# Retention's values and gates of three heads by a seven-product block scheme, the weight sums made by adding DMAs

## The chip, the cores and the metric

The kernel runs on one core of one Trainium2 chip. The metric is the device time of one execution in microseconds, as the median of several runs. A core has TensorE (PE in the profile), which multiplies; VectorE (DVE), ScalarE (ACT) and GpSimd (POOL), which work on tiles element by element; SyncE (SP), which here only issues DMAs; and 16 DMA engines that move data between HBM and on-chip memory. SBUF holds the tiles, PSUM the results of matmuls. Each engine works through its own instructions in program order and waits on semaphores for the others.

## What is computed

An encoder of four layers for one sequence of 512 tokens and a model width of 1024, float32. Layer i mixes tokens by latent attention (i = 0, 3), retention (1) or gated linear attention (2), and then runs a SwiGLU FFN; each sub-layer ends in a LayerNorm of alpha * x + y. The change touches retention alone, which occurs once, with 4 heads, query and key width 256, value and gate width 512:

```python
def retention_mixer(x, positions, w_in, decay_logit, gn_w, gn_b, w_o):
    proj = x @ w_in
    q = proj[..., : H * DK].reshape(B, S, H, DK)
    k = proj[..., H * DK: 2 * H * DK].reshape(B, S, H, DK)
    v = proj[..., 2 * H * DK: 2 * H * DK + H * DV].reshape(B, S, H, DV)
    g = proj[..., 2 * H * DK + H * DV:]
    q = apply_rotary(q, positions)
    k = apply_rotary(k, positions) * (DK ** -0.5)
    log_gamma = jax.nn.log_sigmoid(decay_logit)
    y = (retention_chunked(q, k, v, log_gamma[0], False)
         + flip_seq(retention_chunked(flip_seq(q), flip_seq(k), flip_seq(v), log_gamma[1], True)))
    y = (y - mean(y)) * lax.rsqrt(var(y) + LN_EPS)      # per token and head
    y = y.reshape(B, S, H * DV) * gn_w + gn_b
    return (jax.nn.silu(g) * y) @ w_o
```

The two chunked passes together weight the score of tokens n and m by a power of a decay, gamma^|n-m|, one gamma for each direction.

## The kernel before

**Precision.** Every large product is done in three matmuls. A float32 operand is kept as a pair: `hi`, its cast to the matmul's short float32 form, and `lo`, the rest. `split` (L100 to L102) makes a pair with two instructions, a cast on ACT (L101) and a subtraction on DVE that needs the cast (L102). `mm3` (L124 to L128) adds hi·hi (L126), hi·lo (L127) and lo·hi (L128) in one PSUM tile. A weight comes in pieces of 512 KB: `wload` issues the load into a `wraw` tile on SP's queue (L110; three such tiles) and `wsplit` splits it into `whi` and `wlo` (six tiles each). The layer's input is kept as the pair `xh`, `xl`. PSUM has six tiles for products (`ps`) and two for transposes (`tp`).

**Retention** runs head by head. Each head computes queries and keys (`queries_keys`, 96 matmuls of 128x512) and turns them by the rotary angles on DVE (`rope`, L787 to L789) with a split behind it; the values (`values`, 96 matmuls); the scores (`scores`, 24 matmuls in four tiles, m = 0 to 3, each evicted by one DVE instruction that multiplies by the decays, L863, and then split); the gate (`gate`, 96 matmuls, evicted by ACT with Silu, L876). `mix` multiplies scores and values (48 matmuls), normalizes each token on DVE and ACT, applies gn_w on DVE and gn_b and the gate on POOL (L902, L903). `turn` transposes the result (16 matmuls L910) and `out` multiplies it by the head's rows of w_o (96 matmuls), added to the running sum.

The heads overlap: head h's queries and keys come first, then `turn` of head h-1, values, scores, the decays of head h+1 (`decay`, L849 to L852), gate, mix and only then `out` of head h-1. Head 0 runs values, queries and keys, gate, scores, mix. Within this order a scheduler places each engine's instructions by priority, which is the order in which the code issues them, and by what is ready; `issue_after` holds a block of instructions behind a named one on the same engine. Tiles come from pools with a tag and a number of buffers; a new tile waits until an old one of the tag is read for the last time. The phase of a mixer (L1248) gives the number of buffers per tag; retention has the default, 47 tiles of tag `b` (128x512).

## Time and profile before

| | us |
|---|---|
| median of 3 runs | 2548.4 |
| lowest, highest | 2548.17, 2549.81 |
| the profiled execution's own time | 2547.14 |
| its span in the profile | 2545.4 |
| PE busy in the span | 2523.1 |
| DVE busy | 1771.1 |
| ACT busy | 975.5 |
| POOL busy | 200.9 |

The span is what the profile's records cover; the execution's own time is 1.7 us more. Mean granted clock of PE over the span: 0.998 of full speed. Busy times of different engines overlap. Retention with its output projection lies at about 588 to 1005 us.

### The profile page before, as it was taken

What the parts mean: (1) busy time and instruction counts of PE and PEld (TensorE: products, weight loads), DVE (VectorE), ACT (ScalarE), POOL (GpSimd) and SP (SyncE); (2) the same over time, 40 slices, a digit from 0 to 9 for tenths busy, and PEclk for the clock granted to TensorE, in tenths of its full rate; (3) what the DMA queues carried; (4) which work ended last, traced back from release to release, by engine and by line L of the source; (5) the groups of instructions that cost most, each with busy time, mean ns of one, the idle gap of its engine ahead of it and who ended that gap; (6) DMA issues with size and microseconds to landing.
All of it is one profiled execution on the core that took longest, in us unless ns stands there. A gap on an engine that the chain in (4) does not pass through costs nothing.

```text
span 2545.4 us, 32575 instructions
## 1 busy us (share of the span) xinstructions
PE 2523.1 (99%) x12804; PEld 2148.3 (84%) x12804; DVE 1771.1 (70%) x2988; ACT 975.5 (38%) x1405; POOL 200.9 (8%) x247
## 2 busy tenths in 40 slices
PE   8999999999999999999999999999999999999998
PEld 7888888888888888988888899988888888988887
DVE  6877666658755648666657878866657786666656
ACT  4752433323333332333333665233332564233331
POOL 2000111000100101111100000011100100011101
PEclk9999999999999999999999999999999999999999
DMA  4213333323222323333333222333332312333331
GB/s 153 71 42 104 100 100 99 100 83 108 75 83 76 99 83 100 104 95 100 108 100 88 90 69 75 113 100 99 100 92 76 96 57 64 102 100 99 100 91 58
DMA packets 294714, 232.35 MB, mean 91 GB/s; under 512 B 21121, under 2 KB 244481, under 8 KB 294561
## 3 DMA queue, kind: packets, MB, share of 16 engines
q1 hardware_dynamic: 294560, 230.28, 29.9%
q8 instruction: 100, 1.64, 0.3%
q14 instruction: 54, 0.43, 0.1%
HBM read 228.15 MB, written 2.10 MB: 90 GB/s over the span
## 4 chain that ended last, share of the span: by engine, by line
PE 94%; DVE 3%; ACT 1%; DMA 1%; issue 0%; POOL 0%; SPq 0%; DVEq 0%; ACTq 0%
PE ps L126 30%; PE ps L128 30%; PE ps L127 30%; PE tp L658 1%; PE tp L156 1%; DVE wlo L102 1%; PE ps L639 1%; PE ps L638 0%; ACT whi L101 0%; DMA wraw<-in_ret_w_in 0%; DMA wraw<-in_mla_w_down 0%; DMA wraw<-in_mla_w_uq 0%; ACT b L548 0%; DVE xt L203 0%; PE tp L910 0%
## 5 line engine op out<-in xcount | busy, mean ns | idle before, releaser
L101 ACT CAST whi<-wraw 128x1024 fp32r<-128x1024 f32 (+3 forms) x398 | 412.1, 1040 | 695.4 <-PE ps L127 231.8
L126 PE MATMUL ps<-xh,whi 128*128 128x512 f32 (+1 forms) x1792 | 657.2, 367 | 0.0
L127 PE MATMUL ps<-xl,whi 128*128 128x512 f32 (+1 forms) x1792 | 656.9, 367 | 0.1
L128 PE MATMUL ps<-xh,wlo 128*128 128x512 f32 (+1 forms) x1792 | 656.9, 367 | 0.0
L102 DVE TENSOR_TENSOR wlo<-wraw,whi 128x1024 fp32r<-128x1024 f32 (+3 forms) x398 | 488.6, 1237 | 212.3 <-ACT whi L101 204.3
L126 PEld LDWEIGHTS ps<-xh,whi 128*128 128x128 f32 x1792 | 337.8, 189 | 55.3 <-issue 0.4
L127 PEld LDWEIGHTS ps<-xl,whi 128*128 128x128 f32 x1792 | 338.1, 189 | 54.8 <-DVE lnx L139 0.3
L128 PEld LDWEIGHTS ps<-xh,wlo 128*128 128x128 f32 x1792 | 338.1, 189 | 54.6
L126 PE MATMUL ps<-whi,xh 128*128 128x512 f32 (+3 forms) x752 | 265.1, 353 | 0.7 <-ACT xh L101 0.7
L128 PE MATMUL ps<-whi,xl 128*128 128x512 f32 (+3 forms) x752 | 263.1, 350 | 1.4 <-DVE xl L102 1.4
L127 PE MATMUL ps<-wlo,xh 128*128 128x512 f32 (+3 forms) x752 | 262.8, 349 | 0.1
L180 DVE TENSOR_TENSOR xt<-ps,xt 128x512 f32<-128x512 f32 x288 | 187.4, 684 | 34.9 <-PE ps L128 34.9
L127 PE MATMUL ps<-wlo,fh 128*128 128x512 f32 x448 | 174.4, 389 | 0.0
L128 PE MATMUL ps<-whi,fl 128*128 128x512 f32 x448 | 174.4, 389 | 0.0
L126 PE MATMUL ps<-whi,fh 128*128 128x512 f32 x448 | 174.4, 389 | 0.0
L128 PEld LDWEIGHTS ps<-whi,xl 128*128 128x128 f32 x752 | 143.0, 190 | 19.4 <-DVE xl L102 2.4
L126 PEld LDWEIGHTS ps<-whi,xh 128*128 128x128 f32 x752 | 143.3, 191 | 18.4 <-ACT xh L101 1.1
L127 PEld LDWEIGHTS ps<-wlo,xh 128*128 128x128 f32 x752 | 143.3, 191 | 16.8 <-DVE wlo L102 0.4
L322 DVE TENSOR_TENSOR ft<-ps,b 128x512 f32<-128x512 f32 x64 | 44.2, 691 | 141.6 <-PE ps L128 78.0
L101 ACT CAST whi<-wt 128x1024 fp32r<-128x1024 f32 x64 | 67.5, 1054 | 191.0 <-PE ps L127 134.1
L325 POOL TENSOR_TENSOR ft<-ft 128x256 f32<-128x256 f32 x32 | 23.6, 737 | 1477.9 <-DVE ft L322 1477.9
L102 DVE TENSOR_TENSOR fl<-ft,fh 128x1792 fp32r<-128x1792 f32 x32 | 64.8, 2026 | 91.4 <-ACT fh L101 91.4
(257 smaller groups left out, 3985.5 us busy)
## 6 DMA issues: line engine op xcount, KB each, us to landing
wraw<-in_ffn_w_in SPq DMA_DIRECT2D x176, 512.0 KB, 3.9
wt<-in_ffn_w_out SPq DMA_DIRECT2D x48, 512.0 KB, 4.7
wraw<-in_ret_w_in SPq DMA_DIRECT2D x48, 512.0 KB, 4.0
wraw<-in_ffn_w_out SPq DMA_DIRECT2D x40, 512.0 KB, 3.3
wraw<-in_gla_w_in SPq DMA_DIRECT2D x22, 512.0 KB, 3.6
wraw<-in_mla_w_o SPq DMA_DIRECT2D x16, 512.0 KB, 3.8
wraw<-in_ret_w_o SPq DMA_DIRECT2D x16, 512.0 KB, 4.6
wraw<-in_mla_w_down SPq DMA_DIRECT2D x8, 512.0 KB, 4.3
```

The lines of the kernel that those rows point to most:

```text
L101: a = self.nc.scalar.copy(hi, src)
L102: b = self.nc.vector.tensor_tensor(lo, src, hi.bitcast(F32), op=ALU.subtract)
L126: mm(out, s[0], m[0], start=start, stop=False)
L127: mm(out, s[0], m[1], start=False, stop=False)
L128: mm(out, s[1], m[0], start=False, stop=stop)
L156: nc.tensor.transpose(ps[:, j, :], self.xt[t][:, (4 * g + j) * P : (4 * g + j + 1) * P], self.ident)
L180: nc.vector.tensor_tensor(x, ps, x, op=ALU.add)
L322: nc.vector.tensor_tensor(ft[:, 2:4, :] if f % 2 else ft[:, 1::-1, :], half(pu), half(s), op=ALU.mult)
L325: tt(ft[:, 4, :], ft[:, 0, :], ft[:, 3, :], op=ALU.add)
L639: nc.tensor.matmul(ps, qr[:, sl], krz[e], start=False, stop=True)
L658: nc.tensor.transpose(ps[:, kk, qq, :], pq[qq][:, k * P : (k + 1) * P], self.ident)
```

## The change

Values and gate of a head are one product of x (512 x 1024) with two column blocks of w_in (1024 x 512 each). The code after takes x as 2 x 2 blocks (tokens in halves a, the model width in halves c) and the weights as 2 x 2 blocks (values or gate, width half), and forms the result by the Winograd variant of Strassen's scheme: seven block products and a number of sums in place of eight products. Head 0 stays as it was.

- `factors` makes the sums of blocks of x once, during head 0, on DVE: ten additions or subtractions of 128x1024 in scratch tiles of the tag `t` (two buffers), and four splits into pairs of the tag `s`.
- `values_gate` makes seven `product`s. A product of a single weight block loads it as before into `wraw` tiles; one of a sum of blocks loads the first by SP into two `t` tiles and adds the others to them by DMAs from GpSimd. Its weight splits are held behind the eviction in `put_done`: that of score tile m = 2 for the first product, later that of the previous product's first half.
- Each product is 24 matmuls in two PSUM tiles, evicted by its `put` function: a copy on ACT, or additions on DVE, a split or Silu behind some.
- `out` of head h-1 becomes eight steps of 12 matmuls set between the products; in the last head four of them run behind `mix`, which is followed by the last head's own `out_last`.
- Scores now stand directly behind `turn`, without values between. `mix` works on pairs of token tiles with one `rsqrt_n` for two, and its two POOL operations are on DVE.
- Retention's phase has 30 tiles of tag `b`, 8 of `s`, 2 of `t`.

The core of the diff:

```diff
         def scores(h, q, k, gam):
...
+                if m == 2:
+                    self.put_done = i
...
         def mix(h, at, v, gs):
...
+            for t0 in (0, 2):
...
+                    nc.vector.tensor_tensor(y, y, gw, op=ALU.mult)
+                    nc.vector.tensor_tensor(y, y, gb, op=ALU.add)
+                    nc.vector.tensor_tensor(gs[t], gs[t], y, op=ALU.mult)
...
+        def factors():
...
+            def both(x, y):
+                d, e = scratch(), scratch()
+                tt(d, f32(x[0]), f32(y[0]), op=ALU.subtract)
+                tt(e, f32(x[1]), f32(y[1]), op=ALU.subtract)
+                tt(d, d, e, op=ALU.add)
+                return d
...
+            d = both(a21, a22)
+            s1 = keep(d)
+            for x in a11:
+                tt(d, d, f32(x), op=ALU.subtract)
+            s2 = keep(d)
+            for x in a12:
+                tt(d, d, f32(x), op=ALU.add)
+            s4 = keep(d)
+            return s1, s2, keep(both(a11, a21)), s4, a11, a12, a22
...
+            def product(blocks, s, put):
+                if len(blocks) == 1:
+                    ts = [self.wp.tile([P, 2, 512], F32, tag="wraw", name="wraw", bufs=self.nraw) for _ in range(2)]
+                else:
+                    ts = [self.b((P, 2, 512), name="wt", tag="t") for _ in range(2)]
+                for n, ac in enumerate(blocks):
+                    for c in range(2):
+                        if n:
+                            nc.gpsimd.dma_start(ts[c], block(ac, c), accum_op=ALU.add)
+                        else:
+                            nc.sync.dma_start(ts[c], block(ac, c))
+
+                with self.tc.issue_after(self.put_done.ins):
+                    ws = [self.wsplit(t, 2, 512) for t in ts]
+                for tt in range(2):
+                    ps = self.ps()
+                    for k in range(4):
+                        hi, lo = ws[k // 2]
+                        s2_ = tuple(x[:, k, tt * P : (tt + 1) * P] for x in s)
+                        self.mm3(ps, s2_, (hi[:, k % 2, :], lo[:, k % 2, :]), k == 0, k == 3)
+                    i = put(tt, ps)
+                    if tt == 0:
+                        self.put_done = i
...
+            steps = [
+                ([b21, b22, b12, b11], a22, keep("c21")),
+                ([b11], a11, keep("c11")),
+                ([b22, b12, b11], s2, put6),
+                ([b21], a12, put2),
+                ([b12, b11], s1, put5),
+                ([b22], s4, put3),
+                ([b12, b22], s3, put7),
+            ]
...
             else:
                 q, k = queries_keys(h)
                 yT = turn(gs)
-                v = values(h)
                 at = scores(h, q, k, gam)
                 gam = decay(h + 1) if h + 1 < RET_H else None
-                gs = gate(h)
...
+                v, gs, todo = values_gate(h, fac)
+                outs = out(h - 1, yT)
+                last = h == RET_H - 1
+                for step, n in zip(todo, (0, 0, 1, 1, 1, 1, 0) if last else (1, 2, 1, 1, 2, 1, 0)):
+                    step()
+                    for _ in range(n):
+                        outs.pop(0)()
             mix(h, at, v, gs)
...
-        with self.phase(**({}, {}, {"v": 8, "r": 4})[i % 3]):
+        with self.phase(**({}, {"s": 8, "t": 2, "b": 30}, {"v": 8, "r": 4})[i % 3]):
```

How the instructions stand on the engines is told below at three places; a row gives line, operation, output and inputs, and shape. Numbers behind names tell tiles of one name apart.

First, PE in head 1 behind k's projection. Before (`tp` are the transposes of head 0's result, `ps_6143` is the first tile of values):

```order
L910 MATMUL tp_6092<-ident_75,b_5684 128x128
L910 MATMUL tp_6092<-ident_75,b_5711 128x128
L126 MATMUL ps_6143<-whi_6121,xh_70 128x512
L127 MATMUL ps_6143<-wlo_6122,xh_70 128x512
L128 MATMUL ps_6143<-whi_6121,xl_71 128x512
L126 MATMUL ps_6143<-whi_6121,xh_70 128x512
```

After, the scores `ps_6123` and `ps_6136` stand there (`bh_5994`, `bl_5995` are the pair of q's first half, `bh_6074`, `bl_6075` that of k's, both from `rope`):

```order
L936 MATMUL tp_6096<-ident_75,b_5684 128x128
L936 MATMUL tp_6096<-ident_75,b_5711 128x128
L126 MATMUL ps_6123<-bh_5994,bh_6074 128x512
L127 MATMUL ps_6123<-bl_5995,bh_6074 128x512
L126 MATMUL ps_6136<-bh_5994,bh_6074 128x512
L127 MATMUL ps_6136<-bl_5995,bh_6074 128x512
L128 MATMUL ps_6123<-bh_5994,bl_6075 128x512
L128 MATMUL ps_6136<-bh_5994,bl_6075 128x512
L126 MATMUL ps_6149<-bh_5994,bh_6074 128x512
```

Values' matmuls, which needed only the layer's input and a weight, have gone from between the transposes and the scores.

Second, DVE at head 1's scores. Before (`b_6266` to `b_6305` are the four evictions, L863; `bl` behind each is its low part; `wlo` are weights for later products):

```order
L102 TENSOR_TENSOR bl_6256<-ps_6230,bh_6255 128x512
L863 SCALAR_TENSOR_TENSOR b_6266<-ps_6259,ret_g_5765 128x512
L102 TENSOR_TENSOR wlo_6610<-wraw_6607,whi_6609 128x1024
L102 TENSOR_TENSOR bl_6269<-b_6266,bh_6268 128x512
L863 SCALAR_TENSOR_TENSOR b_6279<-ps_6272,ret_g_5765 128x512
L102 TENSOR_TENSOR bl_6282<-b_6279,bh_6281 128x512
L863 SCALAR_TENSOR_TENSOR b_6292<-ps_6285,ret_g_5765 128x512
L102 TENSOR_TENSOR bl_6295<-b_6292,bh_6294 128x512
L863 SCALAR_TENSOR_TENSOR b_6305<-ps_6298,ret_g_5765 128x512
L849 TENSOR_SCALAR ret_g_6311<-ret_di_5202,rlg_5378 128x448 x2
```

After (the evictions are L880, `b_6130` to `b_6169`; `bl_6111` and `bl_6120` belong to the transposed result; `wlo_6196` and `wlo_6200` are the two halves of the first weight sum, from the `t` tiles `wt_6185` and `wt_6186`):

```order
L102 TENSOR_TENSOR bl_6111<-tp_6105,bh_6110 128x512
L102 TENSOR_TENSOR bl_6120<-tp_6114,bh_6119 128x512
L880 SCALAR_TENSOR_TENSOR b_6130<-ps_6123,ret_g_5765 128x512
L102 TENSOR_TENSOR bl_6133<-b_6130,bh_6132 128x512
L880 SCALAR_TENSOR_TENSOR b_6143<-ps_6136,ret_g_5765 128x512
L102 TENSOR_TENSOR bl_6146<-b_6143,bh_6145 128x512
L880 SCALAR_TENSOR_TENSOR b_6156<-ps_6149,ret_g_5765 128x512
L102 TENSOR_TENSOR wlo_6196<-wt_6185,whi_6195 128x1024
L102 TENSOR_TENSOR bl_6159<-b_6156,bh_6158 128x512
L880 SCALAR_TENSOR_TENSOR b_6169<-ps_6162,ret_g_5765 128x512
L102 TENSOR_TENSOR wlo_6200<-wt_6186,whi_6199 128x1024
L102 TENSOR_TENSOR bl_6172<-b_6169,bh_6171 128x512
```

The low part of the first weight sum now stands behind the third eviction. On PE, these rows are at the end of the scores (`ps_6162` is the fourth score tile, `ps_6245` one of `out`, `ps_6203` the first product):

```order
L126 MATMUL ps_6162<-bh_6003,bh_6083 128x512
L127 MATMUL ps_6162<-bl_6004,bh_6083 128x512
L128 MATMUL ps_6162<-bh_6003,bl_6084 128x512
L126 MATMUL ps_6245<-whi_6235,bh_6092 128x512
L127 MATMUL ps_6203<-wlo_6196,xh_70 128x512
L128 MATMUL ps_6203<-whi_6195,xl_71 128x512
L126 MATMUL ps_6203<-whi_6195,xh_70 128x512
L127 MATMUL ps_6203<-wlo_6196,xh_70 128x512
L128 MATMUL ps_6203<-whi_6195,xl_71 128x512
L126 MATMUL ps_6203<-whi_6199,xh_70 128x512
```

So the first product's second matmul, L127, needs `wlo_6196` from that place on DVE, and everything behind it on PE stands behind it.

Third, ACT at the end of head 0's gate. Before (`b_5711` is the gate's last Silu, `bh_5722` and `bh_5735` the first casts of head 0's scores):

```order
L101 CAST whi_6005<-wraw_6003 128x1024
L101 CAST whi_6036<-wraw_6034 128x1024
L101 CAST whi_6121<-wraw_6119 128x1024
L876 ACTIVATE b_5711<-ps_5686 128x512
L101 CAST whi_6127<-wraw_6125 128x1024
L101 CAST bh_5722<-b_5720 128x512
L101 CAST bh_5735<-b_5733 128x512
```

After:

```order
L101 CAST whi_6009<-wraw_6007 128x1024
L101 CAST whi_6040<-wraw_6038 128x1024
L101 CAST whi_6195<-wt_6185 128x1024
L895 ACTIVATE b_5711<-ps_5686 128x512
L101 CAST whi_6199<-wt_6186 128x1024
L101 CAST bh_5722<-b_5720 128x512
L101 CAST bh_5735<-b_5733 128x512
```

In place of weights that had come by plain loads, the casts of the two halves of head 1's first weight sum, `whi_6195` and `whi_6199`, stand around the last Silu and ahead of the score casts.

## Rows read from the trace of the kernel before

**Rows 1.** Page, parts 1 and 4: each engine's busy us, chain that ended last.

```profile
PE 2523.1 (99%) x12804; PEld 2148.3 (84%) x12804; DVE 1771.1 (70%) x2988; ACT 975.5 (38%) x1405; POOL 200.9 (8%) x247
...
PE 94%; DVE 3%; ACT 1%; DMA 1%; issue 0%; POOL 0%; SPq 0%; DVEq 0%; ACTq 0%
```

**Rows 2.** Windows, heads 1-3: us, PE, PEld, DVE, ACT, POOL, clock, DMA-share, GB/s.

```profile
674.00:779.00 105.00, 105.00 (x473) 87.06 (x472) 69.97 (x135) 37.46 (x47) 22.56 (x16) 1.00 0.21 66
779.00:884.00 105.00, 105.00 (x473) 87.05 (x472) 61.78 (x111) 34.71 (x44) 10.31 (x8) 1.00 0.30 90
884.00:990.00 106.00, 106.00 (x477) 87.93 (x476) 60.13 (x106) 32.18 (x41) 10.34 (x8) 1.00 0.29 90
```

**Rows 3.** Waits of PE, 640 to 1000 us, the largest: total, count, longest.

```profile
PE ps L126 <- ACT bh L101: 0.2, 1, 0.2
```

**Rows 4.** PE timeline, heads 0 and 1: start, us, engine, line, op, tiles.

```profile
663.87 0.50 PE L126 MATMUL ps<-bh 128*128 128x512 f32 x1
...
683.36 0.39 PE L126 MATMUL ps<-xh,whi 128*128 128x512 f32 x1
...
696.05 0.40 PE L128 MATMUL ps<-xh,wlo 128*128 128x512 f32 x1
696.29 1.04 PE L910 MATMUL tp<-ident,b 128*128 128x128 f32 x8
697.08 0.48 PE L126 MATMUL ps<-whi,xh 128*128 128x512 f32 x1
```

**Rows 5.** DVE timeline behind head 1's k; in brackets idle before, releaser.

```profile
696.49 0.69 DVE L788 TENSOR_TENSOR b<-ps,tab 128x512 f32<-128x512 f32 x1 [0.26 <-PE ps L128]
697.21 0.69 DVE L789 TENSOR_TENSOR b<-b 128x512 f32<-128x512 f32 x1
697.82 1.22 DVE L102 TENSOR_TENSOR wlo<-wraw,whi 128x1024 fp32r<-128x1024 f32 x1
699.56 0.69 DVE L787 TENSOR_TENSOR b<-ps,tab 128x512 f32<-128x512 f32 x1
700.16 0.68 DVE L788 TENSOR_TENSOR b<-ps,tab 128x512 f32<-128x512 f32 x1
```

**Rows 6.** Timeline of ACT, the same place.

```profile
697.94 0.62 ACT L101 CAST bh<-b 128x512 fp32r<-128x512 f32 x1 [0.59 <-DVE b L789]
```

**Rows 7.** Timeline of DVE at head 1's scores.

```profile
725.21 0.68 DVE L863 SCALAR_TENSOR_TENSOR b<-ps,ret_g 128x512 f32<-128x512 f32 x1
726.65 0.69 DVE L102 TENSOR_TENSOR bl<-b,bh 128x512 fp32r<-128x512 f32 x1 [0.76 <-ACT bh L101]
727.26 0.68 DVE L863 SCALAR_TENSOR_TENSOR b<-ps,ret_g 128x512 f32<-128x512 f32 x1
...
729.29 0.68 DVE L863 SCALAR_TENSOR_TENSOR b<-ps,ret_g 128x512 f32<-128x512 f32 x1
```

**Rows 8.** Timeline of PE early in layer 0, where it had stood still.

```profile
43.18 0.44 PE L531 MATMUL tp<-ident,b 128*128 128x128 f32 x2 [2.17 <-DVE b L525]
43.37 0.61 PE L127 MATMUL ps<-wlo,xh 128*128 128x512 f32 x1
...
46.77 0.49 PE L126 MATMUL ps<-whi,xh 128*128 128x512 f32 x1
```

**Rows 9.** Windows behind that gap and in head 0 (columns as in rows 2).

```profile
44.00:45.00 1.00, 1.00 (x3) 0.78 (x3) 0.94 (x2) 0.81 (x2) 0.03 (x1) 0.50 1.03 303
7.00:8.00 1.00, 0.93 (x2) 0.48 (x2) 1.00 (x2) 0.34 (x1) 0.00 (x0) 1.00 1.07 366
607.00:642.00 35.00, 35.00 (x156) 29.01 (x155) 28.04 (x63) 13.58 (x17) 0.00 (x0) 1.00 0.39 120
```

**Rows 10.** DMA view of the loads from ret_w_in, 512 KB each.

```profile
DMA to landing us min/median/max: 3.5/4.0/8.1
```

**Rows 11.** Timeline of SP's DMA queue, head 0: start, us, line, tiles, count.

```profile
632.62 29.74 SPq L110 DMA_DIRECT2D wraw<-in_ret_w_in  x6
```

**Rows 12.** Page, part 5: busy us, mean ns | idle before, releaser.

```profile
L101 ACT CAST whi<-wraw 128x1024 fp32r<-128x1024 f32 (+3 forms) x398 | 412.1, 1040 | 695.4 <-PE ps L127 231.8
```

More of the change, by code (lines that the diff above doesn't have):

```diff
@@ L862, in scores @@
                 a = self.b()
-                nc.vector.scalar_tensor_tensor(
+                i = nc.vector.scalar_tensor_tensor(
                     a, ps, RET_DK**-0.5, gam[:, 384 - m * P : 896 - m * P], op0=ALU.mult, op1=ALU.mult
@@ L916, in out, with step @@
         def out(h, yT):
-            last = h == RET_H - 1
-            if last:
-                self.ln_begin(l, 0)
-            st = lambda f, t: (yT[f][0][:, t * P : (t + 1) * P], yT[f][1][:, t * P : (t + 1) * P])
-            self.out_proj(st, wo[h * 512 : (h + 1) * 512], 4, ALPHA if h == 0 else None, last)
+            ch = {}
+            def step(t, hf):
+                if t == 0:
+                    rows = wo[h * 512 : (h + 1) * 512]
+                    ch[hf] = [self.wcols(rows, c * 256, 2, hf * 512, 512) for c in range(2)]
+                ps = self.ps()
+                for f in range(4):
+                    w2 = ch[hf][f // 2]
+                    sl = slice(t * P, (t + 1) * P)
+                    self.mm3(
+                        ps, (yT[f][0][:, sl], yT[f][1][:, sl]), (w2[0][:, f % 2, :], w2[1][:, f % 2, :]), f == 0, f == 3
+                    )
+                self.acc(t, hf, ps, ALPHA if h == 0 else None, False)
@@ new lines, in values_gate, with block, keep, put @@
+        def values_gate(h, fac):
+            rows = w.rearrange("(g a p) c -> g p a c", g=4, p=P)
+            s1, s2, s3, s4, a11, a12, a22 = fac
+            v, gs = [None] * NT, [None] * NT
+            tmp = {}
+            def block(ac, c):
+                c0 = 2048 + ac % 2 * 2048 + h * 512
+                return rows[2 * (ac // 2) + c, :, :, c0 : c0 + 512]
+            def product(blocks, s, put):
[7 more added lines that the diff above has]
+                            nc.gpsimd.dma_start(ts[c], block(ac, c), accum_op=ALU.add)
+                        else:
+                            nc.sync.dma_start(ts[c], block(ac, c))
+                with self.tc.issue_after(self.put_done.ins):
+                    ws = [self.wsplit(t, 2, 512) for t in ts]
+                for tt in range(2):
+                    ps = self.ps()
+                    for k in range(4):
[5 more added lines that the diff above has]
+                        self.put_done = i
+            tt_ = nc.vector.tensor_tensor
+            def keep(name):
+                def put(tt, ps):
+                    tmp[name, tt] = self.b()
+                    return nc.scalar.copy(tmp[name, tt], ps)
+                return put
+            def put_v(t, x):
+                v[t] = self.bpair()
+                self.split(*v[t], x)
+            def put6(tt, ps):
+                u = tmp["u", tt] = self.b()
+                tt_(u, ps, tmp["c11", tt], op=ALU.add)
+                x = tmp["c21", tt]
+                return tt_(x, x, u, op=ALU.add)
+            def put2(tt, ps):
+                x = tmp["c11", tt]
+                i = tt_(x, ps, x, op=ALU.add)
+                put_v(tt, x)
+                return i
+            def put5(tt, ps):
+                u = tmp["u", tt]
+                return tt_(u, ps, u, op=ALU.subtract)
+            def put3(tt, ps):
+                g = gs[tt] = self.b()
+                i = tt_(g, ps, tmp["u", tt], op=ALU.add)
+                nc.scalar.activation(g, g, AF.Silu)
+                return i
+            def put7(tt, ps):
+                x = tmp["c21", tt]
+                tt_(x, ps, x, op=ALU.add)
+                put_v(2 + tt, x)
+                g = gs[2 + tt] = tmp["u", tt]
+                i = tt_(g, g, ps, op=ALU.subtract)
+                nc.scalar.activation(g, g, AF.Silu)
+                return i
+            b11, b12, b21, b22 = range(4)
+            steps = [
[7 more added lines that the diff above has]
+            ]
+            return v, gs, [lambda a=a: product(*a) for a in steps]
@@ L931, in retention @@
                 at = scores(h, q, k, gam)
+                gam = decay(1)
+                fac = factors()
             else:
@@ L934, in retention @@
                 yT = turn(gs)
-                v = values(h)
                 at = scores(h, q, k, gam)
                 gam = decay(h + 1) if h + 1 < RET_H else None
-                gs = gate(h)
-            if h == 0:
-                gam = decay(1)
+                v, gs, todo = values_gate(h, fac)
[5 more added lines that the diff above has]
+                        outs.pop(0)()
             mix(h, at, v, gs)
-            if h:
-                out(h - 1, yT)
-        out(RET_H - 1, turn(gs))
+            if h == RET_H - 1:
+                for step in outs:
+                    step()
+        out_last(RET_H - 1, turn(gs))
     def gla(self, l, j):
```

67 lines of the change are left out of this document (48 added, 19 removed).

## The prediction

> **What bounds the kernel now.** I read the busy table and the chain of work first. TensorE (PE) is busy for 99% of the span, and the chain that ended last runs 94% over it [rows 1]; the reader should see that nothing else bounds the kernel on average. The change lies in retention's heads 1 to 3, so I then read those stretches: in 105 and 106 us PE is busy for 105.00 and 106.00, at full clock, with DVE at 60 to 70 and the DMA engines at a fifth to a third [rows 2]. In that stage PE's waits hold lines no larger than 0.2 us [rows 3]. Heads 1 to 3 are thus saturated on PE: fewer matmuls are worth their full price there, and so is any new wait. The price of one is a spacing, since matmuls overlap: from the start at 683.36 to that at 696.05 there are 56 intervals, (696.05 - 683.36) / 56 = 0.2267 us [rows 4].
>
> **Part 1, matmuls removed.** Values and gate of a head are 2 x 96 matmuls of 128x512. Seven products of 24 make 168, so 24 go per head and 72 in all. 72 x 0.2267 = 16.3 us, all on the path: **-16.3**.
>
> **Part 2, the scores lose their cover.** Before, PE had values' 96 matmuls (21.8 us) between the transposes of `turn` and the scores, and the gate's 96 behind them. Now the scores follow the transposes at once (first order rows of the change), and the first product needs `wlo` of a weight sum that DVE computes only behind the eviction of score tile m=2 (second order rows). I follow DVE from PE's last k matmul, taken as t=0 (696.28 in the trace). There DVE starts the k rope's second multiplication at +0.21 and the sum at +0.93; ACT casts from +1.66 to +2.28 [rows 5, 6]. PE has two groups of transposes meanwhile, 0.8 us (eight start at 696.29, the next matmul at 697.08 [rows 4]), then nothing: the first scores wait 1.4 to 1.5 us for the cast, taken as 1.4. From there DVE takes a 128x512 pass every 0.60 us [rows 5]: low part of k's first half until 2.9, three rope passes to 4.7, the cast to 5.6, its low part and two of the turned tiles' at 5.6 to 7.4, the other two turned tiles at 8.4 and 9.0 behind PE's remaining transposes. So score eviction m=0 starts at 9.6. One score tile costs DVE 2.04 us, because eviction, ACT's cast and the low part follow each other [rows 7]: m=1 at 11.65, m=2 at 13.7, then the weight's low part (1.22 [rows 5]) from 14.3 to 15.5. PE has in that time 16 transposes, 24 score matmuls (5.4 us) and two or three others for which its operands are there; it is through with them at about 9.2, but for one at 10.3. Idle: 15.5 - 9.2 - 0.2 = about 6.1 us, where before there was none.
>
> Then the clock. Behind a gap of 2.17 us early in the trace [rows 8] PE's granted clock is 0.50 (1.2 instead of 2.4 GHz) [rows 9], and the eight matmuls from 43.37 to 46.77 take (46.77 - 43.37) / 8 = 0.425 each, so 8 x (0.425 - 0.227) = 1.6 us more [rows 8]. I charge 1.6 to each long gap. DVE's weight split for `out`, behind the decay's passes, adds 0.3; with the first wait of 1.4: 6.1 + 1.4 + 1.6 + 0.3 = 9.4 per head, **+28.2** for three. Bounds: with the first wait covered and the tiles 0.5 us closer (two spacings, 1.1), 6.9 per head, 21; with one tile more in line before the split (2.04), 11.4 per head, 34.
>
> **Part 3, sums by the loads.** A sum of n blocks is one plain load and n-1 adding DMAs from GpSimd, on two `t` tiles at once. The trace shows no adding DMA. Let A be the time of one adding step of such a pair. Nearest rows: a plain 512 KB load lands in 4.0 us at the median and 8.1 at the longest [rows 10]. An adding DMA has twice the bytes to fetch; 512 KB at the highest throughput seen, 366 GB/s [rows 9], is 1.43 us, so 4.0 + 1.4 = 5.4 and I take A = 5.5, nearer to the median than to the longest since the engines are idle for two thirds here [rows 2]; the range uses A = 4.0 to 8.1. That an adding DMA is below a plain one I exclude: it does the load and more.
>
> The Trainium skill ("DMA: Bandwidth & Descriptors", Anatomy of one DMA — SWDGE (gpsimd) path) gives about 2 us plus the bytes at 436 GB/s; with the bytes doubled that would be an estimated 4.4 us, and the sum below would come to about +18 rather than +26. No run here shows a load from GpSimd.
>
> Where A matters:
> - Head 0 to head 1. The factors of x (ten sums, four splits: 14 DVE passes of 128x1024, 17 us at 1.22 [rows 5]) go to a stretch in which DVE is busy for 28.04 of 35 us [rows 9]; their scratch tiles are the `t` tiles, so these come free at about 637 and 642. The second tile's load is queued on SP behind a weight load (the third of six between 632.6 and 662.4, about 644 [rows 11]); it lands at 648.5. Three adding steps: 665 at A = 5.5. ACT's casts of both sums stand ahead of head 0's score casts (third order rows), so the mix, which began at 663.87 [rows 4], waits for 648.5 + 3A + 1.04 (cast of a weight [rows 12]) + 0.62 (score cast [rows 6]): 667.5, so +3.7, with the clock **+5.3**. At A = 4.0: 662.2, nothing. At 8.1: +10.6 + 1.6.
> - The three-block sum of product 3. Its tiles come free when product 1's split is done; in head 3, where `out` puts no steps there, only 47 matmuls (10.7 us) lie between. Load 4.0, 2A, split 2.2, against 10.7 plus the 0.6 of a pass: a wait of about 2A - 5.1. A = 5.5: 5.9 + 1.6 = **+7.5**. A = 4.0: 2.9 + 1.6. A = 8.1: 11.1 + 1.6. In heads 1 and 2 three `out` steps more (36 matmuls, 8.2 us) lie between: 2A - 12.6 at the most, nothing at 5.5, 3.6 each at 8.1.
> - Product 1 of heads 2 and 3 has some 21 us (72 matmuls, 16.3, and the mix's statistics) for a load and three steps before ACT's casts hold up the mix: 3(A - 5.7), nothing at 5.5, 7.2 each at 8.1.
>
> The Trainium skill (the same page, Issuing engines are not separate DMA queues) says that the transfers of all issuing engines share the same DMA engines, so by it two sums under way and the loads beside them would lengthen each other, toward rival R2. The trace has a DMA share of 0.2 to 0.3 there [rows 2], which leaves room.
>
> **Part 4, the rest.** The mix in pairs moves two passes from GpSimd to DVE (8 x 0.6 = 4.8 us a head; PE is then busy with 12 to 48 matmuls of `out` or the next q, which hide it; uncovered only before the last `turn`, where both tiles' passes stand in line: 1 us, taken with 0 to 2, v's split behind weight splits in it): **+1**. Plain loads stay 512 KB each.
>
> **Sum** at A = 5.5: 28.2 + 5.3 + 7.5 + 1 - 16.3 = +25.7. The profiled execution took 2547.14, the median of the runs is 2548.4, 1.3 above it; 2547.1 + 25.7 = 2572.8 in a profiled run, **2574** as a median.
>
> **Rivals.**
> - *R1, the chain of scores costs less and the change is not slower.* If PE's new idle time stays under 16.3 us in all, that is under 5.4 per head with nothing lost to sums, the matmuls decide. That takes DVE's line before the split to be some 4 us shorter than I have it (the rope's first passes done before k's last matmul, the tiles 0.5 us closer, the clock not falling), and A near 4. For it: DVE is idle for a third of these stretches [rows 2], so it may come to the line with less in hand than I assume. Against: each of the line's links hangs on the one ahead, and the order puts nothing else on PE. With 3 to 5 us per head it is 9 to 15 - 16.3 + 0 to 5 for sums: 2541 to 2552, about 2545.
> - *R2, adding DMAs as slow as the longest load.* A = 8.1: 28.2 + (10.6 + 11.1 + 7.2 + 14.4 + 1.6 x 6 = 52.9) + 1 - 16.3 = +66, **2614**. It decides from A = 5.7, where product 1's chain starts to hold up the mix. For: two at once, beside SP's loads. Against: the share of 0.3.
> - *R3, they cost what a load costs.* A = 4.0: 28.2 + 0 + 4.5 + 1 - 16.3 = +17.4, **2566**.
> - That the matmuls don't go away is no rival: the order lists 72 fewer.
>
> **How the numbers follow.** Within 0.2%, 5.1 us, counts as the same: 2543.3 to 2553.5. Forecast with A from 4.7 to 6 (2568 to 2590): 0.37. R3, with the score chain at its lower bound (2554 to 2568): 0.25. R2 (2590 to 2620): 0.18. R1: 0.20, of which 0.11 is faster and 0.09 the same. So faster 0.11, same 0.09, slower 0.80. For 8 in 10 I leave out R1's faster half and some of the rest (0.15 of it) and the top of R2 (0.05): 2551 to 2608.
>
> **What the profile after would show.** Right: matmuls fewer by 72; in heads 1 to 3 a gap of about 6 us on PE released by DVE's `wlo` from a `wt` tile, with a granted clock of 0.50 behind it; the same matmul spacing elsewhere. GpSimd's adding loads landing 5 to 6 us after the one before; ACT waiting on DMA with `whi` from `wt` at the end of head 0; a gap before product 3 in head 3. Wrong: gaps of under 3 us before product 1 (then Part 2 fails and R1 holds); landings at 4 or 8 (R3, R2); a gap that I have not named, such as evictions of products on DVE behind splits.

## The result, and the profile after

| | before | after |
|---|---|---|
| median, us | 2548.3 (4 runs) | 2705.14 (4 runs) |
| lowest, highest | 2548.17, 2549.81 | 2701.97, 2706.92 |
| span in the profile | 2545.4 | 2700.0 |
| mean granted clock of PE | 0.998 | 0.972 |

The changed kernel is slower by 157 us: a ratio of 1.0613, 95% interval 1.0594 to 1.0631. The prediction was slower, at 2574 in a range of 2551 to 2608; the time lies 97 us above the range. The sign was right and the size was not.

The page after, parts 1, 3, 4 and 6 (to be read against rows 1; `q0` is GpSimd's DMA queue with its packets, MB and share, and the last line gives the adding DMAs, KB each and median us from issue to landing):

```profile
PE 2553.7 (95%) x12732; PEld 2158.1 (80%) x12732; DVE 1826.3 (68%) x3038; ACT 997.3 (37%) x1437; POOL 209.2 (8%) x257
...
q0 software_dynamic: 11424, 22.02, 5.2%
...
PE 82%; DVE 6%; issue 5%; DMA 4%; ACT 3%; POOL 1%; SPq 0%; DVEq 0%; ACTq 0%; POOLq 0%
...
wt<-in_ret_w_in POOLq DMA_DIRECT2D x42, 512.0 KB, 6.2
```

PE has 72 instructions fewer, as the prediction's first step says, and yet 30.6 us more busy time: at the old speed it would have been 16.3 us less, so the matmuls took 46.9 us longer. Most of that is the clock. From 588 to 1180 us the mean granted clock is 0.88; by the trace's record of the clock, PE was busy there for 78.4 us at 0.50, the lower of its two levels, where before it was so for none. Half of it, 39 us, is the price; the other 8 us are not placed.

```profile
588.00:1180.00 592.00, 469.17 (x1952) 373.86 (x1951) 343.50 (x607) 170.19 (x219) 53.88 (x44) 0.88 0.50 122
```

The chain's share on PE fell from 94% to 82%, and DMA, ACT and "issue" came in. The waits of PE and of ACT in retention (588 to 1180 us), largest first, with total, count and longest, where before PE's line was 0.2 us [rows 3]:

```profile
PE ps L126 <- ACT bh L101: 49.2, 9, 24.7
PE ps L126 <- ACT whi L101: 31.7, 9, 11.6
PE ps L127 <- DVE wlo L102: 20.8, 10, 6.1
PE ps L126 <- ACT b L926: 15.5, 2, 8.4
```

```profile
ACT whi L101 <- DMA wt<-in_ret_w_in: 172.6, 21, 20.9
```

The line of ACT is the one to see: ACT stood 172.6 us before casts of weight sums whose DMA had not landed, and the casts of scores, values and mix stand behind them on ACT. That is why the longest wait in PE's largest line, 24.7 us, names `bh`, a score's cast, although no score was late by itself.

I added up all of PE's gaps of 0.3 us and more from 588 to 1180 us: 122.3 us. By what ended them, and where: the end of head 0, 25.0; ahead of products in heads 1 to 3, for a weight or its sum, 37.1; the scores, with the hold behind them, 31.3; the mix's evictions (L926), 15.5; the casts of values at the start of a mix, 12.0; the rest 1.4. With the 46.9 us of longer matmuls that is 169.2. The span grew by 154.6, and 16.3 of matmuls were saved, 170.9 together, so 1.7 us are not placed. The largest gap of each kind, and the clock behind one of them (columns as in rows 2):

```profile
688.34 0.79 PE L126 MATMUL ps<-bh 128*128 128x512 f32 x1 [24.67 <-ACT bh L101]
...
738.83 0.80 PE L127 MATMUL ps<-wlo,xh 128*128 128x512 f32 x1 [4.52 <-DVE wlo L102]
...
1005.85 0.80 PE L126 MATMUL ps<-xh,whi 128*128 128x512 f32 x1 [8.44 <-ACT b L926]
...
1066.23 1.22 PE L126 MATMUL ps<-whi,bh 128*128 128x512 f32 x2 [11.61 <-ACT whi L101]
```

```profile
739.00:740.00 1.00, 1.00 (x3) 0.81 (x4) 1.00 (x3) 0.00 (x0) 0.00 (x0) 0.50 0.13 18
```

And the cause, on GpSimd. Its timeline at the end of head 0 and later in head 1's mix; each row is the issue of one adding DMA of 512 KB:

```profile
661.49 1.21 POOL L1019 DMA_DIRECT2D wt<-in_ret_w_in  x1 [5.17 <-PE ps L128]
667.85 1.22 POOL L1019 DMA_DIRECT2D wt<-in_ret_w_in  x1 [5.15 <-issue]
674.14 1.20 POOL L1019 DMA_DIRECT2D wt<-in_ret_w_in  x1 [5.08 <-issue]
680.59 1.21 POOL L1019 DMA_DIRECT2D wt<-in_ret_w_in  x1 [5.25 <-DMA wt<-in_ret_w_in]
...
819.68 1.22 POOL L1019 DMA_DIRECT2D wt<-in_ret_w_in  x1 [7.54 <-issue]
825.99 1.21 POOL L1019 DMA_DIRECT2D wt<-in_ret_w_in  x1 [5.09 <-issue]
832.56 1.22 POOL L1019 DMA_DIRECT2D wt<-in_ret_w_in  x1 [5.35 <-issue]
```

They start 6.3 to 6.6 us apart, and the page gives 6.2 us from issue to landing: one starts when the one ahead is through. Of the 42, none starts before the one ahead has landed, and 30 start 0.25 to 0.45 us behind that landing. At 825.99 that isn't a wait of the program. This DMA adds to the first tile, whose last DMA was issued at 810.92 and landed at 819.36, and the one at 819.68, which landed at 825.68, is for the other tile; the idle time is put down to "issue". So two tiles were "under way" in the code, and one after the other on the chip. The DMA engines were not full in that time (DMA share 0.64, the last figure but one):

```profile
826.00:850.00 24.00, 19.96 (x83) 16.02 (x82) 4.07 (x16) 1.05 (x1) 4.87 (x4) 0.93 0.64 114
```

A step of a pair took 2 x 6.35 = 12.7 us, where the prediction took 5.5 and at most 8.1.

### The profile page after: what moved, and what is told of

It reads as the page before. It is cut to its first block, busy times and chain, and to the rows that moved or that the text cites. A ratio compares the mean times of both kernels' runs of the same rounds, so it can differ in the third digit from the quotient of the medians.

```text
span 2700.0 us, 32591 instructions
## 1 busy us (share of the span) xinstructions
PE 2553.7 (95%) x12732; PEld 2158.1 (80%) x12732; DVE 1826.3 (68%) x3038; ACT 997.3 (37%) x1437; POOL 209.2 (8%) x257
## 3 DMA queue, kind: packets, MB, share of 16 engines
q0 software_dynamic: 11424, 22.02, 5.2%
## 4 chain that ended last, share of the span: by engine, by line
PE 82%; DVE 6%; issue 5%; DMA 4%; ACT 3%; POOL 1%; SPq 0%; DVEq 0%; ACTq 0%; POOLq 0%
PE ps L126 26%; PE ps L127 26%; PE ps L128 26%; DMA wt<-in_ret_w_in 2%; DVE wlo L102 1%; PE tp L675 1%; DMA wraw<-in_ret_w_in 1%; ACT whi L101 1%; POOL wt L1019 1%; PE tp L173 1%; ACT bh L101 1%; DVE bl L102 1%; DMA wraw<-in_mla_w_down 0%; PE ps L656 0%; PE ps L655 0%
## 5 line engine op out<-in xcount | busy, mean ns | idle before, releaser
L126 PE MATMUL ps<-xh,whi 128*128 128x512 f32 (+1 forms) x1792 | 659.0, 368 | 15.5 <-ACT b L926 15.5
L127 PE MATMUL ps<-xl,whi 128*128 128x512 f32 (+1 forms) x1792 | 658.4, 368 | 0.1
L126 PEld LDWEIGHTS ps<-xh,whi 128*128 128x128 f32 x1792 | 338.6, 189 | 72.2 <-ACT b L926 16.3
L127 PEld LDWEIGHTS ps<-xl,whi 128*128 128x128 f32 x1792 | 339.1, 189 | 55.1 <-DVE lnx L139 0.3
L127 PE MATMUL ps<-wlo,xh 128*128 128x512 f32 (+3 forms) x632 | 220.2, 348 | 15.5 <-DVE wlo L102 15.4
L126 PE MATMUL ps<-whi,xh 128*128 128x512 f32 (+3 forms) x632 | 220.4, 351 | 7.7 <-ACT whi L101 7.0
L101 ACT CAST whi<-wt 128x1024 fp32r<-128x1024 f32 x88 | 92.6, 1052 | 363.6 <-DMA wt<-in_ret_w_in 172.6
L128 PE MATMUL ps<-whi,xl 128*128 128x512 f32 (+3 forms) x632 | 219.2, 347 | 2.3 <-DVE xl L102 2.3
L126 PE MATMUL ps<-whi,bh 128*128 128x512 f32 (+1 forms) x416 | 161.1, 388 | 27.7 <-ACT whi L101 24.7
L126 PE MATMUL ps<-bh 128*128 128x256 f32 (+1 forms) x376 | 129.6, 351 | 50.4 <-ACT bh L101 50.0
L127 PE MATMUL ps<-wlo,fh 128*128 128x512 f32 x448 | 174.3, 389 | 0.0
L102 DVE TENSOR_TENSOR wlo<-wt,whi 128x1024 fp32r<-128x1024 f32 x88 | 114.2, 1298 | 85.1 <-ACT whi L101 84.1
L127 PE MATMUL ps<-wlo,bh 128*128 128x512 f32 (+1 forms) x416 | 160.6, 386 | 5.4 <-DVE wlo L102 5.4
L128 PE MATMUL ps<-whi,bl 128*128 128x512 f32 (+1 forms) x416 | 158.7, 383 | 0.0
L127 PEld LDWEIGHTS ps<-wlo,xh 128*128 128x128 f32 x632 | 122.9, 194 | 30.2 <-DVE wlo L102 17.6
```

What stands on the lines that cost most here:

```text
L101: a = self.nc.scalar.copy(hi, src)
L102: b = self.nc.vector.tensor_tensor(lo, src, hi.bitcast(F32), op=ALU.subtract)
L126: mm(out, s[0], m[0], start=start, stop=False)
L127: mm(out, s[0], m[1], start=False, stop=False)
L128: mm(out, s[1], m[0], start=False, stop=stop)
```

## The experiments

"Measured" is one run, with the kernel before at 2547.5 to 2548.9 beside it, unless an interval is given. e1, e3 and e4 leave the additions out, e2 half of each sum; the others leave nothing out.

**What is slow about the sums: e1 to e4.** e1, plain loads in place of adding ones:

```diff
-                            nc.gpsimd.dma_start(ts[c], block(ac, c), accum_op=ALU.add)
+                            nc.gpsimd.dma_start(ts[c], block(ac, c))
```

> The same DMAs from GpSimd with the same waits, but as plain loads: the later blocks overwrite the first instead of being added to it, so the weight sums are left out of the computation. Theory A (one DMA from GpSimd holds GpSimd for its whole 6.3 us, whatever it does with the data, so the two tiles of a pair follow each other): starts of successive DMAs stay 6.2 to 6.5 us apart where the tiles are free, time within 10 us of 2705. Theory B (the adding makes them long and keeps them apart): spacing falls below 4 us and the time by 80 us or more, toward 2600.

Measured 2607.26. GpSimd's timeline:

```profile
651.10 1.47 POOL L1019 DMA_DIRECT2D wt<-in_ret_w_in  x2 [5.93 <-DMA wt<-in_ret_w_in]
...
797.62 0.73 POOL L1019 DMA_DIRECT2D wt<-in_ret_w_in  x1 [3.48 <-DMA wt<-in_ret_w_in]
798.90 0.72 POOL L1019 DMA_DIRECT2D wt<-in_ret_w_in  x1 [0.55 <-DMA wt<-in_ret_w_in]
```

Two loads are handed on in 1.47 us, back to back, with the same waits; theory A is out and B holds, though the time fell less far for it than with the sums away (e3): 37 us of waiting stay. Plain loads in place of adding ones save 2705 - 2607 = 98 us. One more thing changes with the adding: the same 22.02 MB go in 6048 packets here, against 11424 above. Per DMA that is 128 packets of 4 KB where an adding DMA has 256 of 2 KB, with 16 of 4 bytes beside them in either. So e1 alone does not tell the adding from the number of packets.

```profile
q0 software_dynamic: 6048, 22.02, 2.6%
```

What is left of the gaps on GpSimd is waiting for the DMA ahead on the same tile, as the program asks for.

e2, adding DMAs of half the size, the other half of each sum left out:

```diff
+                            nc.gpsimd.dma_start(ts[c][:, :1], block(ac, c)[:, :1], accum_op=ALU.add)
```

> Each adding DMA moves one of its two rows of 512 columns per partition, 256 KB instead of 512 KB; the other half of each sum is left out. Theory A1 (the time of a GpSimd DMA goes with the number of its pieces): spacing about 3.2 to 3.6 us, landing likewise; by the prediction's sum with a step of 2 x 3.4 = 6.8 us instead of 12.7 the time is about 2600. Theory A2 (most of the 6.3 us is a fixed cost of each DMA): spacing 5 us or more and a time above 2670.

Measured 2610.17, as A1 said, though not for its reason: the spacing isn't half, it is gone.

```profile
652.68 1.75 POOL L1019 DMA_DIRECT2D wt<-in_ret_w_in  x2 [6.45 <-DMA wt<-in_ret_w_in]
...
797.54 0.89 POOL L1019 DMA_DIRECT2D wt<-in_ret_w_in  x1 [3.34 <-DMA wt<-in_ret_w_in]
798.80 0.87 POOL L1019 DMA_DIRECT2D wt<-in_ret_w_in  x1 [0.38 <-DMA wt<-in_ret_w_in]
```

Two adding DMAs of 256 KB go out in 0.87 us each, as e1's loads do in 0.73, and what they wait for is the DMA ahead on the same tile. Landing takes 5.9 us at the median. These are adding DMAs of 128 packets, two at once at the most, and GpSimd does not hold them: it is not the adding by itself.

e3 leaves the additions out altogether, so each sum is its first block alone:

```diff
-                for n, ac in enumerate(blocks):
+                for n, ac in enumerate(blocks[:1]):
```

> The adding DMAs are left out, each sum is its first block alone. All other instructions stay. Theory A (the sums cost all that went past the forecast, the scores cost what Part 2 says): idle of PE at the scores of heads 1 to 3 about 7.5 us each, time 2547 + 28 + 1 - 16 = 2560. Rival C (the mix in pairs, evictions on DVE and held splits cost much by themselves): 2590 or more. Rival D (the scores' waits come from the sums too): 2540 to 2550.

Measured 2570.68. PE's gaps at head 1's scores:

```profile
698.15 0.50 PE L126 MATMUL ps<-bh 128*128 128x512 f32 x1 [1.29 <-ACT bh L101]
706.46 0.47 PE L126 MATMUL ps<-whi,bh 128*128 128x512 f32 x1 [1.10 <-DVE b L880]
711.46 0.79 PE L127 MATMUL ps<-wlo,xh 128*128 128x512 f32 x1 [4.53 <-DVE wlo L102]
```

6.9 us, and 6.9 and 7.4 in heads 2 and 3, where the prediction has 1.4 + 6.1. Theory A's 2560 is 11 us short, so it was right on these gaps and not on what lies around them: 6.1 us of smaller gaps (the mix's start, a late weight) and more half clock.

e4 is e3 with the first product's weight splits free of the hold:

```diff
+                if blocks == [b21, b22, b12, b11]:
+                    ws = [self.wsplit(t, 2, 512) for t in ts]
+                else:
+                    with self.tc.issue_after(self.put_done.ins):
+                        ws = [self.wsplit(t, 2, 512) for t in ts]
```

> As e3_nosum, and the first product's weight splits are no longer held behind the third score eviction. Part 2 of the prediction: the hold is the cause of the wait before the first product, so that wait goes, what is left of the scores' idle time is 1 to 2 us per head, and the time falls by 12 to 20 us against e3_nosum, to 2540 to 2548. Rival: the chain of score evictions is late anyway and the next product waits instead; then it falls by less than 5 us.

Measured 2559.02, 11.7 us below e3, just under what was expected of the hold. (The 2540 to 2548 in the expectation was reckoned from 2560 for e3, before e3 had run.) The gap of 4.5 us before the first product is gone in all three heads. A new one of 1.9, 1.9 and 4.6 us stands before the second product, whose split is held behind the first one's eviction:

```profile
715.70 0.85 PE L126 MATMUL ps<-whi,xh 128*128 128x512 f32 x2 [1.90 <-ACT whi L101]
```

**Other ways to make the sums: e5, e6, e12, e15.** e5 splits each adding DMA into two of 256 KB, nothing left out:

```diff
+                            for b in range(2):
+                                nc.gpsimd.dma_start(ts[c][:, b : b + 1], block(ac, c)[:, b : b + 1], accum_op=ALU.add)
```

> Each adding DMA of 512 KB is replaced by two of 256 KB on the two halves of the same data; nothing is left out. Theory P (an adding DMA of 512 KB alone is so long in pieces that GpSimd can't hand on the next until it is nearly through; one of 256 KB is handed on in 0.9 us, as e2_half showed): starts 0.9 to 1.5 us apart, a step of a pair 6 to 8 us, time 2605 to 2640. Theory Q (what holds GpSimd is the sum of pieces under way, so four of 256 KB are held up as two of 512 KB): the step stays near 12 us and the time above 2680.

Measured 2655.57, between the two theories. e2's 0.87 us hold only as long as few are under way; here four may be, and they don't:

```profile
810.57 0.89 POOL L1020 DMA_DIRECT2D wt<-in_ret_w_in  x1 [1.18 <-issue]
812.73 0.87 POOL L1020 DMA_DIRECT2D wt<-in_ret_w_in  x1 [1.27 <-issue]
815.67 0.86 POOL L1020 DMA_DIRECT2D wt<-in_ret_w_in  x1 [2.06 <-issue]
817.71 0.86 POOL L1020 DMA_DIRECT2D wt<-in_ret_w_in  x1 [1.18 <-issue]
```

Starts are 2.0 to 2.9 us apart, again by "issue". Counted over all 84 DMAs, from issue to landing, never more than three are under way: a fourth starts some 0.3 us behind a landing. So something under way is limited, not the single DMA. e12 cuts them once more, into four of 128 KB with rows of half the length:

```diff
+                                for d in range(2):
+                                    sl = slice(256 * d, 256 * d + 256)
+                                    nc.gpsimd.dma_start(ts[c][:, b, sl], block(ac, c)[:, b, sl], accum_op=ALU.add)
```

> As e5_halves with four adding DMAs of 128 KB in place of two of 256 KB, each of as many rows as before but of half the length. If the time of an adding DMA goes with its bytes: about 1 us each, time within 15 us of e5_halves' 2656. If it goes with its number of rows: about 2 us each as in e5, a step of a pair 16 us, time above 2705.

Measured 2699.91, 44 us above e5 and not within 15, and not above 2705 either: neither expectation came out whole. Starts are 1.3 us apart at the median, which looks like a limit by bytes. The count of DMAs under way says otherwise:

```profile
674.10 0.86 POOL L1022 DMA_DIRECT2D wt<-in_ret_w_in  x1 [0.29 <-issue]
675.28 0.89 POOL L1022 DMA_DIRECT2D wt<-in_ret_w_in  x1 [0.32 <-issue]
...
791.65 2.65 POOL L1022 DMA_DIRECT2D wt<-in_ret_w_in  x3 [5.46 <-DMA wt<-in_ret_w_in]
795.03 0.86 POOL L1022 DMA_DIRECT2D wt<-in_ret_w_in  x1 [0.72 <-issue]
```

From 791.65 three go out before any has landed, and the fourth, at 795.03, starts 0.31 us behind the first one's landing at 794.72. Over all 168 DMAs there are again never more than three under way, although each has half the bytes of e5's; 142 start with two others still under way. What the two runs share is the number of packets of a DMA, 144:

```profile
q0 software_dynamic: 12096, 22.03, 5.0%
q0 software_dynamic: 24192, 22.03, 5.6%
```

The first line is e5's, for 84 DMAs, the second e12's, for 168. So three DMAs of 144 packets may be under way (432), while a fourth (576) waits, and so does a second one of the changed kernel's 272 packets (544). Bytes don't order the runs: 768 KB are under way in e5, and in e12 512 KB are too many. Starts are closer in e12 because a DMA lands sooner, 4.2 us at the median against 6.6. In time this gains little: head 2's first sum takes 40.2 us from its first issue to its last landing in the changed kernel, 28.7 in e5 and 37.9 in e12, the order of the three times.

e15 is the changed kernel with four `t` tiles:

```diff
-        with self.phase(**({}, {"s": 8, "t": 2, "b": 30}, {"v": 8, "r": 4})[i % 3]):
+        with self.phase(**({}, {"s": 8, "t": 4, "b": 26}, {"v": 8, "r": 4})[i % 3]):
```

> The changed kernel with four t tiles instead of two, four tiles of tag b fewer, nothing else. If the cost of the sums is latency (GpSimd can't begin a sum until the one ahead has been split; its 14 DMAs x 6.35 us = 89 us per head would fit into a head), the waits for products 3, 5 and 7 go and only head 0's and the scores' stay: 2600 to 2650. If GpSimd's rate is the limit, above 2680.

Measured 2639.91, 65 us better and inside the first range. ACT's wait for sums falls from 172.6 to 44.4 us and the products' waits nearly go; what stays is the scores with their hold, head 0's end (10.8 us), and now 16.9 and 15.5 us at the mix of heads 1 and 2, where the casts of the next head's first sum stand ahead on ACT:

```profile
ACT whi L101 <- DMA wt<-in_ret_w_in: 44.4, 6, 10.7
```

```profile
815.24 0.80 PE L126 MATMUL ps<-bh 128*128 128x512 f32 x1 [16.89 <-ACT bh L101]
```

So 65 us of the loss came from sums that couldn't begin until two tiles were free, behind the split of the sum ahead or, at head 0, behind the scratch sums of `factors`; the length of each DMA is the same (e15's starts are 6.2 to 6.6 us apart too). What stays is the length of a sum and the place of its casts on ACT.

e6 lets DVE add: the later blocks come by SP into weight tiles.

```diff
-                            nc.gpsimd.dma_start(ts[c], block(ac, c), accum_op=ALU.add)
+                            raw = self.wp.tile([P, 2, 512], F32, tag="wraw", name="wraw", bufs=self.nraw)
+                            nc.sync.dma_start(raw, block(ac, c))
+                            nc.vector.tensor_tensor(ts[c], ts[c], raw, op=ALU.add)
```

> The later blocks of each sum are loaded by SP's queue into weight tiles and added on DVE, 14 passes of 128x1024 per head, 17 us; nothing is left out. Theory A (the GpSimd DMAs alone cost what lies above e3_nosum): ACT's waits for the sums shrink to plain loads, time 2575 to 2600, that is e3_nosum's 2571 plus what DVE's 17 us per head add where it is waited for. Rival (the two tiles and the SP queue are the limit, whoever adds): 2620 or more.

Measured 2578.8, in the range of theory A and 8 us above e3, which makes no sums. The adding DMAs, against sums by DVE, are 126 of the 157 us.

**The scores' cover, and what the matmuls are worth: e7 to e11, e13, e14.** e7 is e6 with the scores behind the second product. The split of the first product is free, that of the second stays behind the first one's eviction, and the steps of `out` come one product later, (0, 1, 2, 1, 2, 1, 1):

```diff
                 q, k = queries_keys(h)
                 yT = turn(gs)
-                at = scores(h, q, k, gam)
...
                     step()
+                    if e == 1:
+                        at = scores(h, q, k, gam)
```

> As e6_dvesum, with products 1 and 2 ahead of the scores and no hold on their splits, so that 48 matmuls, 10.9 us, cover the k rope and the later products the score evictions. If the scores' lost cover is a cost of its own (Part 2), the gaps before the first scores and before product 1 go and the time is 18 to 28 us below e6_dvesum, about 2550 to 2570. Rival: DVE, with 17 us more, is now the engine that is late and the gap moves to product 3: less than 10 us below.

Measured 2562.05, 16.8 us below e6: inside the expected time, at the low end of the expected gain. The gaps at the scores are gone; 2.6 us per head stay before the second product, and 0.5 to 4.1 ahead of the transposes. (The expectation says that neither split is held; the second one's was.) e8 is the same move on e5:

> As e5_halves, with products 1 and 2 ahead of the scores. By Theory P 15 to 25 us below e5_halves, 2590 to 2615; by Theory Q the sums stay late and the move gains under 10 us.

Measured 2609.6, 46 us below e5: inside Theory P's times, with about twice its gain. The move gives the sums more time than I had counted.

e9 is e7 with the first product ahead of `turn`, the second one's split free as well, and the last head's output steps spread otherwise:

```diff
-                yT = turn(gs)
-                outs = out(h - 1, yT)
...
                     step()
+                    if e == 0:
+                        yT = turn(gs0)
+                        outs = out(h - 1, yT)
...
-                if self.put_done is None:
+                if self.put_done is None or blocks == [b11]:
...
-(0, 0, 1, 1, 1, 1, 0) if last
+(0, 1, 1, 1, 2, 1, 1) if last
```

e10 drops all holds:

```diff
-                    with self.tc.issue_after(self.put_done.ins):
-                        ws = [self.wsplit(t, 2, 512) for t in ts]
+                ws = [self.wsplit(t, 2, 512) for t in ts]
```

> As e7_move_dve, but product 1 stands ahead of the transposes, the split of product 2 isn't held either, and the last head has its steps of the output product more evenly. If the remaining gaps of e7 (2.6 us per head behind the transposes, up to 4 us ahead of them, and the half clock behind each) come from these two places, they go: 2544 to 2552, that is about level with the kernel before. Rival: DVE's 17 us of sums per head come late elsewhere: 2556 or more.

> As e9_best_p2 with no split held at all. If the holds keep evictions from waiting behind splits, it is slower than e9 by 2 us or more; if they only delay weights, it is faster by 2 us or more.

Measured 2549.63 (ratio 1.0007, 0.9998 to 1.0016) and 2553.27 (1.002, 1.0011 to 1.003). Both are as expected: e9 is level with the kernel before, and the holds that are left are worth 3.6 us. e9 has one large gap, before the last transposes, where only one step of the output product was left to cover the mix:

```profile
989.03 1.29 PE L934 MATMUL tp<-ident,b 128*128 128x128 f32 x4 [8.47 <-DVE b L927]
```

e11 tests the mix in pairs alone, on the kernel before:

```diff
-            for t in range(NT):
+            for t0 in (0, 2):
...
-                nc.gpsimd.tensor_tensor(y, y, gb, op=ALU.add)
-                nc.gpsimd.tensor_tensor(gs[t], gs[t], y, op=ALU.mult)
+                    nc.vector.tensor_tensor(y, y, gb, op=ALU.add)
+                    nc.vector.tensor_tensor(gs[t], gs[t], y, op=ALU.mult)
```

> The kernel before with the mix in pairs of tiles, one reciprocal root for two, and gate and gn_b on DVE, nothing else changed. Part 4: within 1 us per head, 2547 to 2552. Rival: the six PSUM tiles, two of them held longer, or DVE make PE wait for the mix: 2555 or more.

Measured 2548.97, ratio 1.0001 (0.9991 to 1.0011): nothing, as Part 4 has it.

e13 leaves four steps of the output product behind the last mix, e14 five:

```diff
-(0, 1, 1, 1, 2, 1, 1) if last
+(0, 0, 1, 1, 1, 1, 0) if last
```

> As e9_best_p2, with four steps of the output product of head 2 left behind the last mix, as the changed kernel has them. e9 has one gap of 8.5 us there, ahead of the last transposes. If the 72 matmuls are worth their 16.3 us once no wait takes them back, this gap and the half clock behind it go: 8 to 11 us below e9, 2539 to 2542, a ratio of 0.996 to 0.998 to the kernel before. Rival: the DVE passes of the last mix are late whatever PE does in between: 2546 or more.

> As e13_best_tail with five steps left behind the last mix instead of four. If four steps, 10.9 us, cover the last mix, this is within 1 us of e13; if not, up to 3 us faster.

Measured 2541.77 (0.9973, 0.9962 to 0.9984) and 2541.22 (0.9974, 0.9963 to 0.9984), both 0.3% faster than the kernel before, as expected, and alike. e13's windows over the three heads, columns as in rows 2:

```profile
680.00:790.00 110.00, 110.00 (x493) 90.91 (x493) 97.08 (x151) 43.27 (x55) 0.00 (x0) 1.00 0.56 177
790.00:900.00 110.00, 108.17 (x485) 89.29 (x484) 97.05 (x149) 43.40 (x55) 0.00 (x0) 1.00 0.63 194
900.00:1000.00 100.00, 95.45 (x434) 77.38 (x433) 85.72 (x147) 38.13 (x52) 0.00 (x0) 1.00 0.51 161
```

PE is full again in the first window and nearly so in the others, at clock 1.00, and DVE, at 97 of 110 us, is close to its own limit. The span is 2538.7, 6.7 below before, for 16.3 us of matmuls: 6.8 of the other 9.6 are in gaps of 0.3 us and more, some 3 are not placed.

## Why the prediction was wrong

- **Part 1 held as a count.** 72 matmuls fewer. Their full price was not reached in any run: in e13 PE is busy for 14.6 us less than before (2508.5 against 2523.1), and 6.7 of it reach the span.
- **Part 2 held.** 7.5 us of idle time per head, worked out from DVE's line, against 6.9, 6.9 and 7.4 in e3. The cause named, the split held behind the third eviction, is shown by e4, and the lost cover by e7 to e9. In the changed kernel itself the gaps are 31.3 us and not 22.5, since in heads 2 and 3 the first scores waited 5.7 and 7.0 us: the mix ahead had been held up by sums, and the k rope on DVE behind it.
- **Part 3 failed, in one term.** A was "the time of one adding step of such a pair", 5.5 us in a range of 4.0 to 8.1, from plain loads on SP's queue. One adding DMA landing in 6.2 us is near that; the failed step is that both tiles of a pair were taken to go together. GpSimd holds the second back until the first has landed, 6.35 us each, 12.7 for the pair. (The bytes that the queue counts are not doubled by the adding, 22.02 MB in e1 too; the packets are.) The places where A matters were the right ones. With A = 12.7 the prediction's own line for head 0's end gives 648.5 + 38.1 + 1.7 - 663.9 = 24.4 us, and the trace has 24.7. That it fits so well is luck: the second tile's first load landed at 653.7 and not at 648.5, and five adding DMAs and not six came behind it, as the first tile's first one was done by then. For product 3 its line gives too much (12.8 in heads 1 and 2 and 20.3 in head 3; measured 6.7, 5.9 and 14.6; for heads 1 and 2 its own terms give 2A - 13.3 and not 2A - 12.6), for the first sums of heads 2 and 3 too (21 each; the mix waited 7.1 and 8.4, and the scores and casts behind it some 6 more). All in all its sum would be 28.2 + 24.4 + 20.3 + 25.6 + 42 + 9.6 + 1 - 16.3 = +135, about 2683, still 22 below the measured time. A slip of addition in the forecast is too small to matter: at A = 5.5 the line for head 0's end gives 666.7 and not 667.5, so +2.8 where it has +3.7.
- **The upper bound failed for a reason that can be learnt.** The 8.1 was the slowest landing of one load when others are under way, and the argument "the DMA engines are idle for two thirds" was about the engines. What was short was the issuing side: with nothing of the kind in the trace, the bound from above should have held the case that the DMAs of one queue run one after the other, 2 x 5.4 = 10.8 us for the pair. By the prediction's lines that gives about 2655, nearer, and still 50 us short.
- **The clock was undersized in its count.** I charged 1.6 us for each of five gaps at the forecast and of nine at most; there are 24 of over 1 us. The price held: the 39 us of half clock are 1.6 for each of the 24.
- **Part 4 held.** e11.
- **The rivals.** R2 had the direction and the point "from A = 5.7" where product 1's chain holds up the mix. It pictured DMAs that slow each other, not a queue that takes one at a time, and its price stopped at 8.1. R1 needed under 5.4 us of idle time per head at the scores with nothing lost to sums; e3 has no sums and shows 6.9 to 7.4, and is 22 us slower than the kernel before.
- **The sentences on the Trainium skill.** The estimate of 4.4 us from the Trainium skill ("DMA: Bandwidth & Descriptors", Anatomy of one DMA — SWDGE (gpsimd) path) was further off than the rows: an adding DMA took 6.2 us to land, and the next waited for it. What the Trainium skill says of all issuing engines sharing the DMA engines (the same page, Issuing engines are not separate DMA queues) speaks of the side that was not short here: from 826 to 850 us, with adding DMAs one behind the other, the mean DMA share was 0.64.

What stays open: the reason for the hold. By e5, e12 and the changed kernel it goes with the packets under way, somewhere between 432 and 544, and not with bytes or with the number of DMAs. What holds these packets, why an adding DMA comes in twice as many as a plain load, and whether plain loads from GpSimd meet the same limit, no run here tells: in e1 the two tiles never let more than two, 288 packets, be under way.

## What to carry to other kernels

Price an operation that no trace shows by its issuing queue as well as by its bytes, and let the upper bound be "one after the other". Where an in-order engine casts what a DMA brings, everything behind the cast waits for that DMA too: read the engine that is idle (ACT, 172.6 us), not the tile that PE waits for. Here a scheme that saves matmuls paid off only once each chain of evictions had other matmuls in front of it, and then in part: of 16.3 us saved, e13 keeps 6.7.

## What the runs showed of the hardware

- An adding DMA of 512 KB from GpSimd takes 6.3 us, 83 GB/s, and the next one starts some 0.3 us behind its landing, also for another tile. Plain loads of the same size from the same queue are handed on in 0.72 us each.
- Adding DMAs of 256 KB are handed on in 0.87 us while two are under way, and every 2.1 us at the median when the queue is full (e5); of 128 KB every 1.3 us (e12).
- The queue is full at three adding DMAs of 144 packets, of 256 KB or of 128 KB alike, and at one of 272 packets. A plain load of 512 KB from GpSimd has 144 packets, an adding one 272.
- PE was at the lower clock, 0.50, for 78.4 us of its busy time in retention, behind 24 gaps of over 1 us: 1.6 us a gap.
